# Gate and up products of two feed-forward blocks by Strassen's algorithm, with the gated features passed through DRAM

## The chip, the core and the metric

The kernel runs on one core of a Trainium2 chip. The core has a matrix engine (PE, whose weight loads have a row of their own, PEld), three engines for elementwise work (DVE, ACT and POOL) and a queue for transfers (SP); ACT and POOL issue transfers too. PE writes only to PSUM, and DVE or ACT bring its results to SBUF. The metric is the device time of one run in microseconds (us), the median of several runs.

## What is computed

One layer over 1056 tokens (1024 of a new stream and 32 of a running one), 1024 features wide. A feed-forward block (FFN) stands at either end of the layer and a token mixer between them.

```python
def rms_norm(x, w):
    xf = x.astype(jnp.float32)
    y = xf * lax.rsqrt(jnp.mean(xf * xf, axis=-1, keepdims=True) + RMS_EPS)
    return (y * w.astype(jnp.float32)).astype(x.dtype)
...
def swiglu(h, wg, wu, wd):
    return (jax.nn.silu(h @ wg) * (h @ wu)) @ wd
...
        x = x + 0.5 * swiglu(rms_norm(x, ffn1_norm[l]), ffn1_wg[l], ffn1_wu[l], ffn1_wd[l])
        ...
        x = x + mix.astype(x.dtype)
        x = x + 0.5 * swiglu(rms_norm(x, ffn2_norm[l]), ffn2_wg[l], ffn2_wu[l], ffn2_wd[l])
```

In each FFN, `wg` and `wu` are 1024 x 2816 and `wd` is 2816 x 1024, all in float32. The mixer (a delta rule, sliding-window attention and their projections) is not touched by the change, apart from the layout in which it gets and gives `x`.

## The kernel before

Features lie along the 128 partitions and tokens along the free dimension. The tokens are cut into three chunks of 352 (`CH`, `NC`), the 2816 hidden features into 22 tiles of 128. A float32 operand is written as the sum of two float32r parts (`split`, L158: ACT copies the high part, DVE subtracts it to get the low part), and a product takes three matmuls: high by high, high by low, low by high (L205, L206, L207 in `proj_g`). Weights come in units of 128 x 1024 (`unit_parts`, L147): a transfer on SP into one of two raw buffers `wr`, then the two parts `wh` and `wl`, three buffers each.

`ffn` (L320) goes over six blocks of four or three hidden tiles (`FF_BLOCKS`). In a block it makes, for each hidden tile and chunk, the gate product `pg` and the up product `pu` (8 x 3 matmuls of 352 columns each). A function `swiglu` then brings them to SBUF, gates them and splits the result into `gh` and `gl`. After that the block's down products are added to `x`: 8 output tiles by 3 chunks, each a group of w x 3 matmuls that ends in one DVE addition (L351). Gate, up and down products of a block thus follow each other, and the gated features never leave SBUF.

The norm costs PE no wait: `weigh` (L278) multiplies `x` by the norm's weight alone, and the tokens' factors 1/rms (`factors`, L288) are multiplied into the outputs of the products (`rb`, L334, L337). Before the first FFN the first chunk and the first weight unit are loaded in four pieces each, so that the products begin with the first piece.

PE's order is written by hand: what the code emits for PE runs in that order. The other engines' instructions are put in order by a scheduler, and each engine works off its own queue strictly in that order. `defer` and `tick` place the small matmuls of a norm so many product steps behind the place where they are asked for.

Of the kernel before, what the change touches and what calls it, by code (L numbers as in the profile page):

```python
# [14 lines left out]
P = 128  # L15
# [21 lines left out]
def unit_plan():  # L37
    """The order of the weight units in the packed weights, and the place of each."""
# [5 lines left out]
    def ffn(f):  # L44
        for (f0, w) in FF_BLOCKS:
            for m in range(f0, f0 + w):
                add((f, "g", m))
                add((f, "u", m))
            for u in range(w):
                add((f, "d", f0, u))  # L50
# [25 lines left out]
# columns of the tensors of small constants  # L76
# [27 lines left out]
def body(tc, wp, wba, xin, cst, mcst, bias, sconv, sdn, kcT, vc, y, dn_p, dn_s, convo, ko, vo, ko_s, vo_s):  # L104
# [4 lines left out]
    hp_ = ctx.enter_context(tc.tile_pool(name="hpool", bufs=1))  # L109
    pmm = ctx.enter_context(tc.tile_pool(name="pmm", bufs=3, space=PSUM))  # L110
    psm = ctx.enter_context(tc.tile_pool(name="psm", bufs=1, space=PSUM))
# [35 lines left out]
    def unit_parts(key, n):  # L147
        """The unit's parts of float32r, in n steps."""
# [20 lines left out]
    # work of the other engines behind a product, emitted a step at a time beside the next products  # L169
# [22 lines left out]
    first = []      # banks beside those of pmm, for the first products of all  # L192
    def proj_g(ws, hi, lo, c):
        """The product of the stationary tiles ws (unit, slot) with chunk c; yields between tiles."""
        if hi[0][c] is None:
            flush()
        bank = first.pop(0) if first else None
        if bank:
            ps = psm.tile([P, CH], F32, name=nm("pm"), tag=bank, bufs=1)
        else:  # L200
            ps = pmm.tile([P, CH], F32, name=nm("pm"), tag="pm")
# [28 lines left out]
    def squares(xc, tp, by):  # L230
        """The sum of the squares of the tiles xc, by the engines named: V with ACT, P alone, or both adding."""
# [17 lines left out]
    def rmsnorm(xc, wname, c, hi, lo, tp, n0, n1):  # L249
        """hi[k][c], lo[k][c] = the parts of RMSNorm of the chunk xc[k]."""  # L250
# [27 lines left out]
    def weigh(xc, wname, c, hi, lo, ks=range(KD)):  # L278
        """hi[k][c], lo[k][c] = the parts of x times the norm's weight."""
        wv = C(wname)  # L280
        for k in ks:
            hi[k][c], lo[k][c] = htile(F32R), htile(F32R)
            nc.scalar.activation(hi[k][c], xc[k], AF.Copy, scale=wv[:, k:k + 1])  # L283
            nc.vector.scalar_tensor_tensor(out=lo[k][c], in0=xc[k], scalar=wv[:, k:k + 1], in1=hi[k][c].bitcast(F32), op0=ALU.mult, op1=ALU.subtract)  # L284

    wait = {}       # by chunk, what follows its factors

    def factors(xc, c, tp, n0, n1, by):  # L288
        """The tile that gets the tokens' factors 1 / rms along the free dim, for the products' outputs."""
        rb = tp.tile([P, CH], F32, name=nm("rb"), tag="rb", bufs=NC)  # L290
        acc = squares(xc, tp, by)
        st = {}
        wait[c] = []

        def sums():
            ps = psm.tile([P, 4], F32, name=nm("pss"), tag="pc", bufs=2)
            for q in range(4):
                nc.tensor.matmul(out=ps[:QB, q:q + 1], lhsT=acc[:, q * QB:(q + 1) * QB], rhs=ones, start=True, stop=True)
            r = tp.tile([P, 4], F32, name=nm("r"), tag="r", bufs=2)
            nc.scalar.activation(r[:QB], ps[:QB], AF.Sqrt, scale=1.0 / (KD * P), bias=epst[:QB])  # L300
            nc.vector.reciprocal(r[:QB], r[:QB])
            st["r"] = r

        def spread():
            r = st["r"]
            pr = psm.tile([P, CH], F32, name=nm("pss"), tag="pd", bufs=1)
            for q in range(4):
                nc.tensor.matmul(out=pr[:, q * QB:(q + 1) * QB], lhsT=r[:QB, q:q + 1].to_broadcast([QB, P]), rhs=ident[:QB, :QB], start=True, stop=True)
            nc.scalar.activation(rb, pr, AF.Copy)
            for f in wait.pop(c):  # L310
                f()

        defer(n0, sums)
        defer(n1, spread)
        return rb

# [3 lines left out]
    def ffn(f, x, hi, lo, tp, gp, done, rb=None):  # L320
        """x += 0.5 SwiGLU(h); done(c) follows a chunk's last addition."""
        for bi, (f0, w) in enumerate(FF_BLOCKS):
# [29 lines left out]
            if not last:  # L352
                wds = []
                for d in range(KD):
                    while len(wds) * 8 < (d + 1) * w:
                        wds.append(load_unit((f, "d", f0, len(wds))))
# [899 lines left out]
```

## Time and profile before

| | |
|---|---|
| median of 3 runs | 2479.81 us (2479.49 to 2480.68) |
| span of the profiled execution | 2480.8 us |
| PE busy | 2459.2 us, 99% of the span, 15803 matmuls |
| PEld busy | 2401.1 us, 97% |
| DVE, ACT, POOL busy | 1094.3, 778.8, 284.5 us |
| float32r matmuls of 352 columns, gate and up of both FFNs | 6336 |
| the same, down products of both FFNs | 3168 |

Matmuls are pipelined, and their rows overlap in time: a row of 0.32 us does not mean that PE does one in 0.32 us. The pace is read from the distance of the starts. A span on POOL is rough.

### The profile page before, as it was taken

How to read it: one execution, taken by the hardware profiler on the slowest of the kernel's cores; microseconds unless marked ns; L12 is line 12 of the kernel's file. 1: busy time of each engine (PE TensorE's matmuls, PEld its weight loads, DVE VectorE, ACT ScalarE, POOL GpSimd, SP SyncE). 2: the span in 40 equal slices, each digit the busy share in tenths (PEclk: the TensorE clock that was granted, in tenths of full speed). 3: DMA queues.
4: the chain of work that ended last, by engine and by line, in shares of the span. 5: the costliest groups of instructions: out<-in, count | busy, mean ns of one | idle time of the engine just before them, and what ended most of it. 6: DMA issues, size and time to landing. Idle time of an engine off the chain costs nothing.

```text
span 2480.8 us, 37935 instructions
## 1 busy us (share of the span) xinstructions
PE 2459.2 (99%) x15803; PEld 2401.1 (97%) x15803; DVE 1094.3 (44%) x2471; ACT 778.8 (31%) x1483; POOL 284.5 (11%) x425
## 2 busy tenths in 40 slices
PE   8999999999999999999999999999999999999999
PEld 8999999999999989999888899999999999999999
DVE  5333333333437678765566632435233333333333
ACT  7212121111124655543586731315112111121111
POOL 0101010100014224222000000001101010010000
PEclk9999999999999999999999999999999999999999
DMA  3111111111113100010000021121111111111112
GB/s 133 52 52 36 51 52 43 43 52 43 52 35 118 54 26 20 21 32 20 20 27 27 27 74 52 35 100 41 43 52 43 52 43 44 42 52 43 52 36 86
DMA packets 34123, 119.24 MB, mean 48 GB/s; under 512 B 3792, under 2 KB 7200, under 8 KB 33568
## 3 DMA queue, kind: packets, MB, share of 16 engines
q1 hardware_dynamic: 31392, 104.97, 12.7%
q0 software_dynamic: 1696, 9.69, 1.0%
q8 instruction: 124, 2.03, 0.3%
q10 hardware_dynamic: 864, 2.16, 0.2%
q14 instruction: 47, 0.39, 0.0%
HBM read 107.43 MB, written 9.38 MB: 47 GB/s over the span
## 4 chain that ended last, share of the span: by engine, by line
PE 95%; DVE 2%; ACT 2%; issue 1%; DMA 0%; POOL 0%; POOLq 0%; ACTq 0%; SPq 0%; DVEq 0%
PE pm L205 29%; PE pm L207 28%; PE pm L206 28%; PE pss L682 1%; PE pss L690 1%; PE pss L1004 1%; PE pss L993 1%; PE pss L968 1%; PE pss L501 1%; PE pss L1044 1%; DVE tc L651 0%; ACT h L283 0%; ACT sq L241 0%; PE pss L736 0%; PE pss L724 0%
## 5 line engine op out<-in xcount | busy, mean ns | idle before, releaser
L205 PE MATMUL pm<-h,wh 128*128 128x352 f32 x3216 | 1061.6, 330 | 8.0 <-ACT wh L160 7.4
L207 PE MATMUL pm<-h,wl 128*128 128x352 f32 x3216 | 1039.7, 323 | 0.0
L206 PE MATMUL pm<-h,wh 128*128 128x352 f32 x3216 | 1037.7, 323 | 0.9 <-DVE h L284 0.9
L205 PEld LDWEIGHTS pm<-h,wh 128*128 128x128 f32 x3216 | 607.0, 189 | 14.7 <-ACT wh L160 7.4
L206 PEld LDWEIGHTS pm<-h,wh 128*128 128x128 f32 x3216 | 608.3, 189 | 3.2 <-DVE h L284 2.6
L207 PEld LDWEIGHTS pm<-h,wl 128*128 128x128 f32 x3216 | 605.0, 188 | 0.0
L160 ACT ACTIVATE wh<-wr 128x1024 fp32r<-128x1024 f32 (+1 forms) x190 | 197.6, 1042 | 662.2 <-PE pm L206 547.4
L205 PE MATMUL pm<-gh,wh 128*128 128x352 f32 x1056 | 341.9, 324 | 0.0
L207 PE MATMUL pm<-gh,wl 128*128 128x352 f32 x1056 | 340.2, 322 | 0.0
L206 PE MATMUL pm<-gl,wh 128*128 128x352 f32 x1056 | 340.0, 322 | 0.0
L161 DVE TENSOR_TENSOR wl<-wr,wh 128x1024 fp32r<-128x1024 f32 (+1 forms) x190 | 251.2, 1324 | 102.6 <-ACT wh L160 100.7
L338 POOL TENSOR_TENSOR s<-s,u 128x352 f32<-128x352 f32 x132 | 125.8, 953 | 1352.2 <-DVE u L337 1296.8
L351 DVE SCALAR_TENSOR_TENSOR x<-pm,x 128x352 f32<-128x352 f32 x288 | 149.9, 523 | 271.0 <-PE pm L207 271.0
L337 DVE TENSOR_TENSOR u<-pm,rb 128x352 f32<-128x352 f32 x132 | 69.2, 524 | 355.8 <-PE pm L207 355.8
L206 PEld LDWEIGHTS pm<-gl,wh 128*128 128x128 f32 x1056 | 199.0, 188 | 0.0
L207 PEld LDWEIGHTS pm<-gh,wl 128*128 128x128 f32 x1056 | 198.3, 188 | 0.0
L205 PEld LDWEIGHTS pm<-gh,wh 128*128 128x128 f32 x1056 | 198.2, 188 | 0.0
L160 ACT ACTIVATE gh<-s 128x352 fp32r<-128x352 f32 x132 | 65.8, 498 | 408.3 <-POOL s L338 408.3
L161 DVE TENSOR_TENSOR gl<-s,gh 128x352 fp32r<-128x352 f32 x132 | 68.8, 521 | 151.4 <-ACT gh L160 151.4
L334 DVE TENSOR_TENSOR s<-pm,rb 128x352 f32<-128x352 f32 x132 | 69.2, 524 | 139.2 <-PE pm L207 137.0
L335 ACT ACTIVATE s<-s 128x352 f32<-128x352 f32 x132 | 64.8, 492 | 200.8 <-DVE s L334 200.8
L546 DVE SCALAR_TENSOR_TENSOR row<-z,cs,row 128x352 f32<-128x352 f32 (+2 forms) x144 | 74.3, 540 | 12.3 <-ACT row L544 11.3
(259 smaller groups left out, 2068.6 us busy)
## 6 DMA issues: line engine op xcount, KB each, us to landing
wr<-wp SPq DMA_DIRECT2D x184, 512.0 KB, 3.4
xs<-x POOLq DMA_DIRECT2D x3, 1408.0 KB, 5.1
x<-xs POOLq DMA_DIRECT2D x6, 704.0 KB, 7.7
x<-xin SPq DMA_DIRECT2D x4, 704.0 KB, 7.7
x<-xin SPq DMA_DIRECT2D x4, 352.0 KB, 5.4
y<-x ACTq DMA_DIRECT2D x2, 704.0 KB, 3.1
y<-x SPq DMA_DIRECT2D x2, 704.0 KB, 3.1
y<-x ACTq DMA_DIRECT2D x4, 176.0 KB, 1.8
```

What stands on the lines that cost most here:

```text
L160: nc.scalar.activation(h, src, AF.Copy)
L161: (eng or nc.vector).tensor_tensor(out=l, in0=src, in1=h.bitcast(F32), op=ALU.subtract)
L205: nc.tensor.matmul(out=ps, lhsT=a, rhs=hi[k][c], start=k == 0, stop=False)
L206: nc.tensor.matmul(out=ps, lhsT=a, rhs=lo[k][c], start=False, stop=False)
L207: nc.tensor.matmul(out=ps, lhsT=b, rhs=hi[k][c], start=False, stop=k == n - 1)
L334: nc.vector.tensor_tensor(out=s, in0=pg, in1=rb[c], op=ALU.mult)
L335: nc.scalar.activation(s, s, AF.Silu)
L337: nc.vector.tensor_tensor(out=u, in0=pu, in1=rb[c], op=ALU.mult)
L338: nc.gpsimd.tensor_tensor(out=s, in0=s, in1=u, op=ALU.mult)
L351: nc.vector.scalar_tensor_tensor(out=x[d][c], in0=ps, scalar=0.5, in1=x[d][c], op0=ALU.mult, op1=ALU.add)
L501: nc.tensor.matmul(out=p1[p0:p0 + m, i, :], lhsT=src[:, o:o + m], rhs=w, start=True, stop=True)
L546: nc.vector.scalar_tensor_tensor(out=o, in0=z[:, z0 + i:z0 + i + m], scalar=cw[:, i:i + 1], in1=o, op0=ALU.mult, op1=ALU.add)
```

## The change

The 22 hidden tiles are taken in 11 pairs, the 1056 tokens in four quarters of 264 (`QT`), the 1024 input features in two halves. For a pair of tiles and a pair of quarters, the gate product is a product of 2 x 2 blocks (two hidden tiles by two halves; two halves by two quarters). For the pairs 1 to 10 it is made with 7 block products in place of 8, by Strassen's algorithm in Winograd's form; the up product likewise. The first pair is multiplied in the ordinary way while the quarters are still being normed.

Each FFN is now two phases. Phase one (`first_quarters`, `ffn_a`) makes all the gated features and stores them to DRAM (`gds`), from POOL's queue. Phase two (`ffn_b`) loads them again on SP, splits them and makes the down products as before, over seven blocks of 4, 3, 3, 3, 3, 3, 3 tiles. Differences of the weights' blocks (`pair_weights`) and of the tokens' quarters (`differences`) are made on DVE and POOL before the split; the additions behind the block products (`products`) are seven DVE instructions over 528 elements. The norm is applied to the quarters themselves before the products (`norm_quarter`); the factors on the outputs are gone. SBUF and PSUM pools are closed and opened anew between the phases, the second phase of the first FFN loads `x` again from the input, and the residual goes through a second DRAM copy (`xs2`) around phase one of the second FFN.

```diff
-FF_BLOCKS = [(0, 4), (4, 4), (8, 4), (12, 4), (16, 3), (19, 3)]
+FF_BLOCKS = [(0, 4)] + [(4 + 3 * i, 3) for i in range(6)]
+NJ = NF // 2
+QT = NT // 4
...
+    def pair_weights(f, j, s):
+        raw = pair_raw(f, j, s)
+        def tt(eng, out, a, b, op):
+            eng.tensor_tensor(out=raw[:, out], in0=raw[:, a], in1=raw[:, b], op=op)
+        a11, a12 = pair_parts(raw, (A11, A12))
+        tt(nc.vector, A11, A11, A21, ALU.subtract)
+        tt(nc.vector, S2, A22, A11, ALU.subtract)
+        tt(nc.gpsimd, A21, A21, A22, ALU.add)
+        s2, s1 = pair_parts(raw, (S2, A21))
+        tt(nc.gpsimd, A12, A12, S2, ALU.subtract)
+        s3, s4 = pair_parts(raw, (A11, A12))
+        a22, = pair_parts(raw, (A22,))
+        return dict(P1=a11, P2=a12, P6=s2, P5=s1, P7=s3, P3=s4, P4=a22)
...
+    def slot(w, hb, key):
+        wh, wl, o = w[key]
+        bank = pf.tile([P, 2, 512], F32, name=nm("pf"), tag="f")
+        for p in range(2):
+            for k in range(4):
+                a, b = wh[:, o + k * P:o + (k + 1) * P], wl[:, o + k * P:o + (k + 1) * P]
+                xh, xl = (t[:, k % 2, p, :] for t in hb[BLK[key]][k // 2])
+                out = bank[:, p, :QT]
+                nc.tensor.matmul(out=out, lhsT=a, rhs=xh, start=k == 0, stop=False)
+                nc.tensor.matmul(out=out, lhsT=a, rhs=xl, start=False, stop=False)
+                nc.tensor.matmul(out=out, lhsT=b, rhs=xh, start=False, stop=k == 3)
+                tick()
+        return bank[:, :, :QT]
...
+        t = slot(w, hb, "P1")
+        nc.scalar.activation(o[0][0], t, AF.Copy)
+        nc.scalar.activation(o[1][0], t, AF.Copy)
+        add(o[0][0], o[0][0], slot(w, hb, "P2"))
...
+        add(o[1][0], o[1][0], slot(w, hb, "P6"))
+        add(o[1][1], o[1][0], slot(w, hb, "P5"))
+        add(o[0][1], o[1][1], slot(w, hb, "P3"))
...
+        t = slot(w, hb, "P7")
+        add(o[1][0], o[1][0], t)
+        add(o[1][1], o[1][1], t)
...
+        add(o[1][0], o[1][0], slot(w, hb, "P4"))
...
+        for j in range(1, NJ):
+            g, u = outs(tp), outs(tp)
...
+            def up(m, h):
+                (nc.gpsimd if m == 0 else nc.vector).tensor_tensor(out=g[m][h], in0=g[m][h], in1=u[m][h], op=ALU.mult)
+                nc.gpsimd.dma_start(out=gd[2 * j + m, h], in_=g[m][h])
+            products(pair_weights(f, j, 0), hb, g, gate_)
+            products(pair_weights(f, j, 1), hb, u, up)
...
+                raw = gp.tile([P, NT], F32, name=nm("gr"), tag="gr", bufs=3)
+                for h in range(2):
+                    nc.sync.dma_start(out=raw.rearrange("p (a h t) -> p a h t", a=2, h=2)[:, :, h, :], in_=gd[f0 + m, h])
+                h, l = (gp.tile([P, NT], F32R, name=nm("gs"), tag="gs", bufs=11) for _ in range(2))
+                split(h, l, raw)
```

PE's queue inside the first FFN, before: gate and up products of 352 columns, high and low parts of `x` as `h`, of the weights as `wh` and `wl`.

```order
L205 MATMUL pm_245<-h_99,wh_94 128x352
L206 MATMUL pm_245<-h_100,wh_94 128x352
L207 MATMUL pm_245<-h_99,wl_95 128x352
L205 MATMUL pm_245<-h_103,wh_94 128x352
L206 MATMUL pm_245<-h_104,wh_94 128x352
L207 MATMUL pm_245<-h_103,wl_95 128x352
```

The same engine now, at the passage from block product P5 to P3 of the second pair (`hb` are the quarters' blocks and their differences, `pf` the PSUM tile of a block product).

```order
L421 MATMUL pf_930<-hb_122,wh_833 128x264
L422 MATMUL pf_930<-hb_123,wh_833 128x264
L423 MATMUL pf_930<-hb_122,wl_834 128x264
L421 MATMUL pf_956<-hb_128,wh_840 128x264
L422 MATMUL pf_956<-hb_129,wh_840 128x264
L423 MATMUL pf_956<-hb_128,wl_841 128x264
```

A matmul has three quarters of the columns, still with a weight load of its own; a pair's gate or up product is 168 of them (7 block products x 2 x 4 x 3), where it was 144 of 352 columns.

ACT's queue at the start of the program, before: the split of the first chunk (L283), squares for the norm (L241) and the split of the first unit (L160), mixed.

```order
L283 ACTIVATE h_99<-x_89,cs 128x352
L241 ACTIVATE sq_222<-x_89 128x352
L160 ACTIVATE wh_94<-wr_93 128x256
L283 ACTIVATE h_103<-x_89,cs 128x352
L241 ACTIVATE sq_224<-x_89 128x352
L283 ACTIVATE h_111<-x_89,cs 128x352
```

ACT's queue at the start now (`raw` are weight pieces as loaded, `t` the quarters of `x`, `hb` the normed and split quarter).

```order
L158 ACTIVATE wh_162<-raw_140 128x512 x2
L158 ACTIVATE wh_168<-raw_145 128x512 x2
L158 ACTIVATE wh_156<-raw_145 128x512
L550 DMA t_96<-xin 128x2x264
...
L550 DMA t_107<-xin 128x2x264
L346 ACTIVATE sq_186<-t_92 128x528
L346 ACTIVATE sq_188<-t_93 128x528
```

The split of eight weight pieces and the issue of twelve transfers of later quarters now stand ahead of the first square, and the first product needs the whole norm of the first quarter.

DVE's queue where the first FFN goes over from products to down products, before: `swiglu`'s L334 and L337, the last split of `gl`, then the additions of the down products.

```order
L334 TENSOR_TENSOR s_1083<-pm_1033,rb_438 128x352
L161 TENSOR_TENSOR wl_1185<-wr_1183,wh_1184 128x1024
L337 TENSOR_TENSOR u_1086<-pm_1058,rb_438 128x352
L161 TENSOR_TENSOR wl_1275<-wr_1273,wh_1274 128x1024
L161 TENSOR_TENSOR gl_1090<-s_1083,gh_1089 128x352
L351 SCALAR_TENSOR_TENSOR x_89<-pm_1099,x_89 128x352
```

DVE's queue now, at the joint of the two phases (`gr` are the gated features as loaded, `gs` their parts, `pf_5226` the last block product of phase one).

```order
L430 TENSOR_TENSOR t_4816<-t_4816,pf_5197 128x528
L430 TENSOR_TENSOR t_4817<-t_4817,pf_5197 128x528
L159 TENSOR_TENSOR wl_5406<-wr_5404,wh_5405 128x1024
L485 TENSOR_TENSOR t_4813<-t_4813,t_4817 128x528
L430 TENSOR_TENSOR t_4816<-t_4816,pf_5226 128x528
L159 TENSOR_TENSOR gs_5311<-gr_5307,gs_5310 128x1056
L485 TENSOR_TENSOR t_4812<-t_4812,t_4816 128x528
L159 TENSOR_TENSOR wl_5496<-wr_5494,wh_5495 128x1024
L505 SCALAR_TENSOR_TENSOR x_5274<-pm_5320,x_5274 128x352
```

The split of the fourth hidden tile of the first block (`gs_5311`) stands behind the addition of the last block product, so a part of the first down product's input comes after the end of phase one.

## Rows read from the trace of the kernel before

**Rows 1.** The page: busy time and share of the span, the chain of work that ended last by engine, and its first lines.

```profile
PE 2459.2 (99%) x15803; PEld 2401.1 (97%) x15803; DVE 1094.3 (44%) x2471; ACT 778.8 (31%) x1483; POOL 284.5 (11%) x425
...
PE 95%; DVE 2%; ACT 2%; issue 1%; DMA 0%; POOL 0%; POOLq 0%; ACTq 0%; SPq 0%; DVEq 0%
```

**Rows 2.** Groups of PE's matmuls by line and shape: busy time, mean ns of one, idle time before them and its releaser. `h` are gate, up and the mixer's products, `gh` and `gl` the down products.

```profile
L205 PE MATMUL pm<-h,wh 128*128 128x352 f32 x3216 | 1061.6, 330 | 8.0 <-ACT wh L160 7.4 <-DVE s L334 0.6
L207 PE MATMUL pm<-h,wl 128*128 128x352 f32 x3216 | 1039.7, 323 | 0.0
L206 PE MATMUL pm<-h,wh 128*128 128x352 f32 x3216 | 1037.7, 323 | 0.9 <-DVE h L284 0.9
L205 PE MATMUL pm<-gh,wh 128*128 128x352 f32 x1056 | 341.9, 324 | 0.0
```

**Rows 3.** Stretches of the span: start and end, length, busy time of PE, PEld, DVE, ACT and POOL with their instructions, granted clock, share of the transfer engines, GB/s.

```profile
0.00:100.00 100.00, 91.10 (x561) 88.67 (x562) 50.18 (x94) 52.00 (x97) 10.86 (x16) 1.00 0.30 104
200.00:400.00 200.00, 200.00 (x1248) 200.00 (x1247) 69.32 (x105) 36.85 (x55) 17.91 (x19) 1.00 0.14 48
```

**Rows 4.** Timeline of PE from 299.71 us on: start, length, line and shape; the first rows and the last row of one line.

```profile
299.87 0.33 PE L205 MATMUL pm<-h,wh 128*128 128x352 f32 x1
300.03 0.32 PE L206 MATMUL pm<-h,wh 128*128 128x352 f32 x1
300.19 0.32 PE L207 MATMUL pm<-h,wl 128*128 128x352 f32 x1
...
302.75 0.33 PE L205 MATMUL pm<-h,wh 128*128 128x352 f32 x1
```

**Rows 5.** Timeline of the weight loads at the same place.

```profile
299.87 0.19 PEld L206 LDWEIGHTS pm<-h,wh 128*128 128x128 f32 x1
300.04 0.19 PEld L207 LDWEIGHTS pm<-h,wl 128*128 128x128 f32 x1
300.19 0.19 PEld L205 LDWEIGHTS pm<-h,wh 128*128 128x128 f32 x1
```

**Rows 6.** Timeline of PE in the mixer: matmuls of 352 columns whose weights are 16 columns wide (128*16), the first and the last of a run of 15.

```profile
804.08 0.32 PE L450 MATMUL pss<-h,wb 128*16 128x352 f32 x1
...
806.33 0.32 PE L450 MATMUL pss<-h,wb 128*16 128x352 f32 x1
```

**Rows 7.** Timeline of PE around the small matmuls of one chunk's norm: eight with one moving column (weights 88 wide), later eight with 88 moving columns (weights 128 wide), each with the product that follows.

```profile
25.89 0.71 PE L298 MATMUL pss<-cs,acc 128*88 128x1 f32 x8
26.47 0.41 PE L205 MATMUL pm<-h,wh 128*128 128x352 f32 x1
...
31.81 1.02 PE L308 MATMUL pss<-cs,r 88*128 88x88 f32 x8
32.62 0.41 PE L205 MATMUL pm<-h,wh 128*128 128x352 f32 x1
```

**Rows 8.** Timeline of the first 14 us: SP's issues, ACT's and DVE's work on 512 columns, and PE's first product.

```profile
0.75 0.39 SPq L373 DMA_DIRECT2D x<-xin  x1
1.19 0.42 SPq L154 DMA_DIRECT2D wr<-wp  x1
...
7.40 0.66 PE L205 MATMUL pm<-h,wh 128*128 128x352 f32 x1 [7.40 <-ACT wh L160]
...
13.16 0.69 DVE L161 TENSOR_TENSOR wl<-wr,wh 128x512 fp32r<-128x512 f32 x1
13.22 0.62 ACT L160 ACTIVATE wh<-wr 128x512 fp32r<-128x512 f32 x1
```

**Rows 9.** Two of the same stretches as in Rows 3, shorter.

```profile
5.00:10.00 5.00, 2.60 (x9) 2.47 (x10) 3.14 (x7) 3.93 (x10) 0.00 (x0) 1.00 1.03 359
10.00:15.00 5.00, 4.65 (x19) 3.66 (x19) 5.00 (x12) 5.00 (x13) 0.00 (x0) 1.00 1.03 420
```

**Rows 10.** Groups of DVE, ACT and POOL by line and shape: busy time, mean ns of one, idle time before them and what ended it.

```profile
L351 DVE SCALAR_TENSOR_TENSOR x<-pm,x 128x352 f32<-128x352 f32 x288 | 149.9, 523 | 271.0 <-PE pm L207 271.0
L694 DVE TENSOR_TENSOR TT<-TT,pss 128x512 f32<-128x512 f32 x16 | 10.9, 684 | 8.9 <-PE pss L692 8.7
...
L160 ACT ACTIVATE gh<-s 128x352 fp32r<-128x352 f32 x132 | 65.8, 498 | 408.3 <-POOL s L338 408.3
L551 ACT ACT_TABLE_LOAD x11 | 14.1, 1283 | 0.2
...
L338 POOL TENSOR_TENSOR s<-s,u 128x352 f32<-128x352 f32 x132 | 125.8, 953 | 1352.2 <-DVE u L337 1296.8 <-ACT s L335 44.9 <-ACT wh L160 7.1
```

**Rows 11.** Timeline of DVE near the end of the second FFN: two splits of the same shape, the second of them beside a POOL instruction.

```profile
2439.72 1.23 DVE L161 TENSOR_TENSOR wl<-wr,wh 128x1024 fp32r<-128x1024 f32 x1 [0.41 <-ACT wh L160]
...
2443.66 1.74 DVE L161 TENSOR_TENSOR wl<-wr,wh 128x1024 fp32r<-128x1024 f32 x1 [0.46 <-ACT wh L160]
```

**Rows 12.** Transfers by line: queue, count, KB each, median us from issue to landing.

```profile
wr<-wp SPq DMA_DIRECT2D x184, 512.0 KB, 3.4
...
x<-xs POOLq DMA_DIRECT2D x6, 704.0 KB, 7.7
...
x<-xin SPq DMA_DIRECT2D x4, 352.0 KB, 5.4
```

**Rows 13.** Stretches as in Rows 3, at the end of the first FFN and at the beginning of the second one's products.

```profile
780.00:800.00 20.00, 18.86 (x117) 18.57 (x116) 17.90 (x36) 9.63 (x22) 14.35 (x23) 0.95 0.49 166
...
1680.00:1700.00 20.00, 20.00 (x134) 20.00 (x132) 13.83 (x28) 15.38 (x31) 3.96 (x4) 1.00 0.00 0
```

More of the change, by code (lines that the diff above doesn't have):

```diff
@@ L196, in proj_g @@
             flush()
[L197 to L201, printed above, removed]
+        ps = pmm.tile([P, CH], F32, name=nm("pm"), tag="pm")
         n = len(ws)
@@ L276, in rmsnorm @@
         defer(n1, scale)
[L278 to L315, printed above, removed]
@@ new lines, in qdiff, with differences @@
+    def qdiff(xq, out, a, b):
+        for i in range(2):
+            eng = nc.gpsimd if i else nc.vector
+            eng.tensor_tensor(out=xq[out[0]][out[1] + i], in0=xq[a[0]][a[1] + i], in1=xq[b[0]][b[1] + i], op=ALU.subtract)
+    def differences(hb, xq, p):
+        q, r = 2 * p, 2 * p + 1
+        qdiff(xq, (q, 0), (r, 0), (q, 0))
+        qdiff(xq, (r, 0), (r, 2), (r, 0))
+        qdiff(xq, (r, 2), (r, 2), (q, 0))
+        qdiff(xq, (q, 2), (q, 2), (r, 2))
+        qparts(hb, xq, "T1", q, 0, "VP")
+        qparts(hb, xq, "T4", q, 2, "VP")
+        qparts(hb, xq, "T3", r, 0, "VP")
@@ new lines, in starter, with start, then, rest @@
+    def starter(hb, xq, wname, tp):
+        def start(q, n0, n1, late=None):
+            def then():
+                qparts(hb, xq, "T2" if q % 2 else "B11", q, 0)
+                if late is not None:
+                    late.append(rest)
+                else:
+                    rest()
+            def rest():
+                qparts(hb, xq, "B22" if q % 2 else "B21", q, 2)
+                if q % 2:
+                    differences(hb, xq, q // 2)
+            norm_quarter(xq[q], wname, tp, n0, n1, then)
+        return start
@@ L359, in ffn @@
             else:
[L360 removed]
+                wds = [load_unit((f + 1, "d", f0, u)) for u in range(w)]
                 for c in range(NC):
@@ new lines, in body, with fetch_q @@
+    st_w, wqp = pool("wqa1")
+    st_v, wqb = pool("wqb1")
+    st_t, tp = pool("t1", "right")
+    st_p, pf = pool("pf1", space=PSUM, bufs=3)
+    st_n, psn = pool("pn1", space=PSUM)
+    psn_tags, psn_bufs = ("na", "nb"), (1, 1)
+    xq = quarters(tp)
+    hb = {}
+    new_blocks(hb, wqp, ("B11", "B21", "T2"))
+    new_blocks(hb, wqb, ("T1", "T3", "B22", "T4"))
+    def fetch_q(q):
+        for a in range(4):
+            nc.scalar.dma_start(out=xq[q][a], in_=xin[a][:, :, q * QT:(q + 1) * QT])
@@ new lines, in body @@
+    fetch_q(0)
+    fw = first_weights(0)
+    for q in range(1, 4):
+        fetch_q(q)
+    start = starter(hb, xq, "n1", tp)
+    start(0, 0, 0)
+    flush()
+    first_quarters(fw, hb, xq, tp, gds[0], lambda q: start(q + 1, 4, 11) if q < 3 else None)
+    ffn_a(0, hb, tp, gds[0])
+    st_n.close()
+    st_p.close()
+    st_t.close()
+    st_v.close()
+    st_w.close()
+    st_h, hp_ = pool("hpool", "right")
+    st_p, pmm = pool("pmm1", space=PSUM, bufs=3)
+    st_n, psm = pool("psm1", space=PSUM)
@@ L1121, in body @@
     ws = [load_unit(("out", d)) for d in (5, 6, 7)]
-    rb = []
+    psn, psn_tags, psn_bufs = psm, ("pc", "pd"), (2, 1)
+    late = []
+    begin = starter(hb, xq, "n3", tp)
     for c in range(NC):
```

275 lines of the change are left out of this document (186 added, 89 removed).

## The prediction

> **What bounds the kernel now.** I read the page's totals first: PE is busy 99% of the span and makes up 95% of the chain that ended last [rows 1]. Then the groups of PE by shape: in the feed-forward blocks the idle time before matmuls is a few microseconds in all [rows 2], and a stretch of 200 us holds 1248 matmuls with PE and its weight loads busy throughout, while DVE is at 35% and ACT at 18% [rows 3]. So the time is the number of matmuls times their pace. The pace is not the 323 ns of a row but the distance of the starts: from 299.87 to 302.75 us there are 18 matmuls of 352 columns, 160.0 ns each [rows 4], at a granted clock of 1.00, which is the level of 2.4 GHz [rows 3]. The last question is what the 160.0 ns consist of, since the change alters the width. A matmul whose weights are only 16 columns wide keeps the same pace (14 steps in 2.25 us, 161 ns) [rows 6]: the weight load does not set it. One column per cycle at 2.4 GHz would be 352 / 2.4 = 146.7 ns, so 13.3 ns are left over, either a fixed sum per matmul or something that grows with the columns. The trace of before can't tell which, as all its float32r matmuls have 352 columns.
>
> **The products.** Removed: gate and up of both FFNs, 2 x 44 x 8 x 3 x 3 = 6336 matmuls x 160.0 ns = 1013.8 us. Added: a pair's gate or up product takes 7 block products x 2 x 4 x 3 = 168 matmuls, ten pairs x 2 x 168 = 3360 in an FFN, and the first pair in the ordinary way 4 quarters x 96 = 384; for two FFNs 7488 matmuls of 264 columns. Their pace is the largest unknown. If the left-over 13.3 ns are fixed, it is 264 / 2.4 + 13.3 = 123.3 ns and the sum 923.3 us; if all of it goes with the columns, 264 / 352 x 160.0 = 120.0 ns and 898.6 us. The nearest rows with short matmuls give a floor: eight with 88 moving columns and 128 weight columns take 0.81 us, some 101 to 108 ns each [rows 7], below both. I take the middle, 121.7 ns and 911.3 us, since nothing decides: **-102.5 us** (-115.2 to -90.5).
>
> The Trainium skill speaks against this change: its page Perfetto Trace Analysis, section Identifying the Most-Contended Engine, judges PE's headroom by the busy share of the weight loads. Here that is 97%, and the change raises the loads from 6336 to 7488; what that would give is the second rival below. The page TensorE: Matmul & The Clock Gate, section Back-to-back issue gap, gives the width over 2.4 GHz plus 2.5 ns; by it the 264-column sum would be 842 us, but it also gives 149.2 ns for 352 columns, where the rows have 160.0, so I don't use it.
>
> **What runs beside phase one.** For each gate or up product of a pair (168 x 121.7 = 20.4 us of PE), DVE does 7 splits and 2 differences of 512 elements at 0.69 us [rows 8], and 7 additions from PSUM of 528, a little over the 0.684 us of a 512-element one [rows 10], say 0.70: 6.2 + 4.9 = 11.1 us, and 0.7 us of gating on average. ACT does 7 copies at 0.62 us and 4 more of 528: 7 us. POOL makes 2 block sums, about 1.4 us each by 953 ns for 352 elements [rows 10], and on average one gating product. All are under PE's 20.4 us, and weights of the next product can be split while this one runs, since there are three buffers. A DVE split beside POOL took 1.74 us instead of 1.23 [rows 11]; were everything on DVE slower by that ratio, it would have 16.7 us of work, still covered. The stores to DRAM (1.1 MB a pair) and loads of weights (2.1 MB a pair, in 41 us) are small against 359 GB/s [rows 9]. I count nothing; if the cover is gone, it is the third rival.
>
> **The start.** Before, the first product begins at 7.40 us [rows 8]. By 100 us 513 products and 48 small matmuls have run [rows 3]; at 160.0 ns, and 0.58 and 0.81 us for eight small ones [rows 7], that is 86.3 us of work, so 13.7 us are lost. Now the first product needs the complete norm of a quarter, and ACT's queue puts other things first. Eight weight pieces and the quarter, 3.2 MB, come at the 359 to 420 GB/s of this stretch [rows 9] by about 12 us; the last of the eight splits ends near 13. Twelve issues at 0.44 us [rows 8] make 5 us, and since later ones wait for the landing of earlier ones (5.4 us for a similar piece [rows 12]), the squares begin at 18 to 21 us. Then in sequence: four squares with their additions 5 us, a table load of 1.28 us [rows 10], root, reciprocal and small matmuls 2.5 us, eight scalings on DVE at 0.43 us (by 523 ns for 352 columns [rows 10]) 3.4 us, the first split 1.3 us: the first products run at 31 to 34 us, and the first quarter's go at DVE's pace of splits for some 4 us more. In all about 35 us are lost against 13.7: **+21 us**. Bounds: 27 lost if the transfers don't delay ACT, 45 if DVE and ACT, which have to norm, split and subtract each later quarter in the 11.7 us of PE's work on the one before, keep PE waiting as well: +13 to +31.
>
> **The norms' small matmuls.** Per quarter 12 with one column and 6 that spread, 1.5 us by [rows 7], eight quarters 12.4 us; before six chunks at 1.4 us, 8.4 us: **+4 us**.
>
> **The joints of the phases.** The first down product needs a PSUM bank that the last addition of phase one empties, and the fourth tile's split stands behind that addition on DVE: 0.7 + 1.4 us, and the queue ahead of it. I take 2 us for each FFN, **+4 us** (0 to 12; the upper end is one load of `x` at 7.7 us [rows 12] that comes late because POOL issues it behind the last stores, less the first products' 1.9 us each).
>
> **The second FFN's start.** Before, PE does not idle there [rows 13]. Now the quarters' norms run beside the output projection; at its end DVE still has eight scalings and two splits ahead of the additions that empty the banks, about 2.5 us, and the gating of the first quarter's products waits for the differences, since both use the same tiles: **+5 us** (0 to 12).
>
> **The rest.** Down products are the same 3168 matmuls; at a block's end the split of the next tile's low part has 1.1 to 1.6 us before it is needed and takes 1.3, about even. The mixer's start, where PE already loses about 1 us and the clock is at 0.95 [rows 13], gets four stores on POOL for each chunk instead of one: **+2 us** (0 to 5).
>
> **The sum.** 2480.8 - 102.5 + 21 + 4 + 4 + 5 + 2 = 2414.3 us of span; the median is 1.0 us under the profiled span, so **2413 us**. With all the low ends 2382, with all the high ends 2453.
>
> **Rivals.**
> First, *the pace is right but the edges cost more*: the norms at the starts and the joints lose PE more than the high ends say. DVE's work for two quarters (16 scalings, 8 to 16 splits, additions, differences) comes near the 24 us that PE takes for them. If it takes half as much again at both starts, 12 us each, the sum is about 2437, and with the high ends of the rest 2465. Chance 0.10 above my range.
>
> Second, *the weight load sets the pace*, and fewer columns don't help. For it speaks that PEld is busy 97% [rows 1] and a load's row is 0.19 us long, more than the pace [rows 5]. Against it speak the loads 16 columns wide at the same pace [rows 6] and the small matmuls at some 105 ns with full loads [rows 7]; a load also begins before the one ahead has ended [rows 5]. If a load and its matmul took 160 ns whatever the width, phase one would be 7488 x 160.0 = 1198.1 us, and the time 2480.8 + 184.3 + 36 - 1 = 2700. The change loses from a pace of (1013.8 - 36) / 7488 = 130.6 ns on. Chance 0.06. The skill's rule on load busy time is this case, and the trace of before bears it out little.
>
> Third, *DVE is late inside phase one*: a block product's bank must be emptied within two products, 5.9 us, but DVE's queue also holds splits that wait for weight buffers. A wait of 1 us in each of 2 x 20 products costs 40 us (2453), 2.5 us costs 100 us and takes the gain away (2513). Against it stand the 11.8 us of work in 20.4. Chance 0.05, half of it at or above the time before.
>
> Fourth, *everything costs less*: the proportional pace and a start at its low end, under 2382. Chance 0.02.
>
> **How the numbers follow.** My forecast, 2413 us, has 0.77 within 2382 to 2453; above it lie the first rival (0.10), the second (0.06) and the third (0.05), below it the fourth (0.02). The range is 2382 to 2453. A measurement of this kernel tells 0.2%, about 5 us, from no change. Faster by more than that holds for the forecast, the first and fourth rivals and half of the third: 0.91; within 0.2%: 0.02; slower: 0.07.
>
> **What would show it.** In the profile of the changed kernel, the starts of 264-column matmuls should be 120 to 123 ns apart in the middle of phase one, with PE busy throughout; a pace of 131 or more would make the prediction wrong in sign. The first product should begin at 31 to 34 us. At the two joints PE should idle about 2 us each with DVE's split or addition as the releaser, and in the first 50 us of both phases one the waits should name DVE and ACT. DVE should be busy some 60% of phase one. Waits on DVE spread evenly through phase one would be the third rival.

## The result, and the profile after

| | us | ratio to before, 95% interval |
|---|---|---|
| before, measured beside it | 2480.17 (median of 4) | 1 |
| after | 2448.57 (2446.24 to 2450.5, 4 runs) | 0.9873 [0.9859, 0.9887] |
| the profiled execution of after | span 2446.0 | |
| forecast | 2413 (2382 to 2453) | |

The change gains 31.6 us where 67 were forecast; the time lies in the range, 36 us above its likeliest value. The page of after, totals, two lines of slices and the chain, answers to [rows 1]:

```profile
span 2446.0 us, 41679 instructions
...
PE 2373.2 (97%) x17003; PEld 2314.3 (95%) x17003; DVE 1348.5 (55%) x2888; ACT 886.7 (36%) x1639; POOL 466.9 (19%) x571
...
PE   4899999999999999999999999999999999999999
...
PEclk9899999999999999999999999999999999999999
...
PE 91%; DVE 4%; ACT 1%; DMA 1%; issue 1%; POOL 1%; SPq 0%; ACTq 0%; DVEq 0%; POOLq 0%
```

DVE has 4% of the chain that ended last instead of 2%, and PE's first two slices (61 us each) are not full. Stretches of after (start and end, length, busy time of PE, PEld, DVE, ACT, POOL with their instructions, granted clock, transfers' share, GB/s) answer to [rows 3]:

```profile
0.00:140.00 140.00, 96.17 (x716) 94.92 (x717) 76.34 (x127) 58.45 (x99) 36.19 (x30) 0.95 0.27 92
60.00:80.00 20.00, 11.85 (x81) 11.66 (x81) 12.22 (x24) 12.45 (x21) 4.12 (x4) 0.81 0.00 1
80.00:100.00 20.00, 19.82 (x144) 19.86 (x145) 12.87 (x19) 6.59 (x11) 9.30 (x6) 0.84 0.05 18
300.00:400.00 100.00, 100.00 (x820) 100.00 (x819) 53.93 (x85) 30.36 (x52) 30.88 (x28) 1.00 0.24 86
520.00:540.00 20.00, 18.16 (x103) 18.19 (x104) 11.11 (x16) 3.31 (x4) 4.78 (x9) 0.91 1.01 375
1700.00:1720.00 20.00, 13.18 (x75) 12.71 (x75) 15.03 (x29) 8.22 (x16) 8.77 (x6) 0.77 0.36 134
1720.00:1740.00 20.00, 20.00 (x154) 20.00 (x153) 14.82 (x24) 10.03 (x17) 5.74 (x4) 0.88 0.00 1
```

The same first 140 us of the kernel before:

```profile
0.00:140.00 140.00, 131.10 (x811) 128.67 (x812) 65.72 (x118) 57.62 (x104) 12.76 (x18) 1.00 0.26 89
```

TensorE idles 43.8 us there instead of 8.9, and what it does it does at a mean clock of 0.95. In the middle of phase one nothing is lost. PE's timeline of after, two of its early products first, then what answers to [rows 4]:

```profile
38.56 0.42 PE L396 MATMUL pf<-hb,wr 128*128 128x264 f32 x1
38.78 0.42 PE L397 MATMUL pf<-hb,wr 128*128 128x264 f32 x1
...
299.68 0.28 PE L421 MATMUL pf<-hb,wh 128*128 128x264 f32 x1
299.80 0.29 PE L422 MATMUL pf<-hb,wh 128*128 128x264 f32 x1
299.92 0.28 PE L423 MATMUL pf<-hb,wl 128*128 128x264 f32 x1
...
302.97 0.29 PE L421 MATMUL pf<-hb,wh 128*128 128x264 f32 x1
...
518.82 0.29 PE L423 MATMUL pf<-hb,wl 128*128 128x264 f32 x1
521.84 0.40 PE L198 MATMUL pm<-gs,wh 128*128 128x352 f32 x1 [2.73 <-DVE t L430]
```

From 299.68 to 302.97 there are 27 steps, 121.9 ns each (forecast 121.7); by the 820 matmuls of 100 us it is 122.0. The early two are 220 ns apart. The last two rows are the first joint: phase one ends at 519.1, and the first down product waits 2.73 us for an addition on DVE. PE's waits of after in the first 130 us, by what it waited for (us in all, times, the longest):

```profile
PE pss L357 <- DVE sq L350: 33.0, 2, 29.9
PE pss L366 <- DVE r L360: 6.1, 2, 5.5
PE pf L397 <- DVE hb L159: 1.8, 1, 1.8
PE pf L396 <- ACT hb L158: 1.7, 1, 1.7
```

And ACT's timeline there (an ACTq row is the issue of transfers):

```profile
10.83 2.71 ACT L158 ACTIVATE wh<-raw 128x512 fp32r<-128x512 f32 x5 [0.48 <-DMA raw<-wq]
13.45 0.55 ACTq L550 DMA_DIRECT2D t<-xin  x1
...
14.04 11.01 ACTq L550 DMA_DIRECT2D t<-xin  x11
25.09 1.18 ACT L346 ACTIVATE sq<-t 128x528 f32<-128x528 f32 x2 [11.02 <-issue]
...
55.37 1.28 ACT L472 ACT_TABLE_LOAD   x1
61.55 0.39 ACT L472 ACTIVATE t<-pf 128x264 f32<-128x264 f32 x1 [4.89 <-POOL hb L159]
...
64.59 0.26 ACT L359 ACTIVATE r<-pss,epst 88x3 f32<-88x3 f32 x1
```

Two places are to be seen. Eleven issues hold ACT for 11.01 us ahead of the first square, so that the first sum reaches TensorE at 29.90. And the first Silu (L472), whose output takes the buffer of a quarter still being subtracted, waits until 61.55 for POOL; the root of the third quarter (L359) is queued behind it, and TensorE waits 5.5 us for its reciprocal.

### The profile page after: what moved, and what is told of

The parts are those of the page before. It is cut to its first block, busy times and chain, and to the rows that moved or that the text cites. A ratio compares the mean times of both kernels' runs of the same rounds, so it can differ in the third digit from the quotient of the medians.

```text
span 2446.0 us, 41679 instructions
## 1 busy us (share of the span) xinstructions
PE 2373.2 (97%) x17003; PEld 2314.3 (95%) x17003; DVE 1348.5 (55%) x2888; ACT 886.7 (36%) x1639; POOL 466.9 (19%) x571
## 4 chain that ended last, share of the span: by engine, by line
PE 91%; DVE 4%; ACT 1%; DMA 1%; issue 1%; POOL 1%; SPq 0%; ACTq 0%; DVEq 0%; POOLq 0%
PE pm L198 15%; PE pm L199 15%; PE pm L200 15%; PE pf L423 11%; PE pf L421 11%; PE pf L422 11%; PE pf L396 1%; PE pf L397 1%; PE pss L852 1%; PE pf L398 1%; PE pss L860 1%; PE pss L1174 1%; PE pss L1163 1%; PE pss L1138 1%; PE pss L671 1%
## 5 line engine op out<-in xcount | busy, mean ns | idle before, releaser
L423 PE MATMUL pf<-hb,wl 128*128 128x264 f32 x2240 | 641.2, 286 | 0.0
L421 PE MATMUL pf<-hb,wh 128*128 128x264 f32 x2240 | 637.1, 284 | 1.3 <-DVE t L473 1.3
L422 PE MATMUL pf<-hb,wh 128*128 128x264 f32 x2240 | 637.8, 285 | 0.0
L421 PEld LDWEIGHTS pf<-hb,wh 128*128 128x128 f32 x2240 | 423.3, 189 | 1.6 <-DVE t L473 1.6
L422 PEld LDWEIGHTS pf<-hb,wh 128*128 128x128 f32 x2240 | 420.9, 188 | 0.0
L423 PEld LDWEIGHTS pf<-hb,wl 128*128 128x128 f32 x2240 | 420.8, 188 | 0.0
L198 PE MATMUL pm<-h,wh 128*128 128x352 f32 x1104 | 372.7, 338 | 1.9 <-DVE t L1293 1.9
L200 PE MATMUL pm<-h,wl 128*128 128x352 f32 x1104 | 357.2, 324 | 0.0
L199 PE MATMUL pm<-h,wh 128*128 128x352 f32 x1104 | 357.1, 323 | 0.0
L198 PE MATMUL pm<-gs,wh 128*128 128x352 f32 x1056 | 344.2, 326 | 7.4 <-DVE t L430 5.2
L199 PE MATMUL pm<-gs,wh 128*128 128x352 f32 x1056 | 342.5, 324 | 0.0
L198 PEld LDWEIGHTS pm<-h,wh 128*128 128x128 f32 x1104 | 208.6, 189 | 8.9 <-issue 6.5
L199 PEld LDWEIGHTS pm<-h,wh 128*128 128x128 f32 x1104 | 208.6, 189 | 0.2
L200 PEld LDWEIGHTS pm<-h,wl 128*128 128x128 f32 x1104 | 208.0, 188 | 0.0
L198 PEld LDWEIGHTS pm<-gs,wh 128*128 128x128 f32 x1056 | 199.9, 189 | 8.0 <-issue 5.5
L199 PEld LDWEIGHTS pm<-gs,wh 128*128 128x128 f32 x1056 | 200.4, 190 | 0.4 <-DVE gs L159 0.4
```

Of the source, the lines that this page charges most:

```text
L198: nc.tensor.matmul(out=ps, lhsT=a, rhs=hi[k][c], start=k == 0, stop=False)
L199: nc.tensor.matmul(out=ps, lhsT=a, rhs=lo[k][c], start=False, stop=False)
L200: nc.tensor.matmul(out=ps, lhsT=b, rhs=hi[k][c], start=False, stop=k == n - 1)
L421: nc.tensor.matmul(out=out, lhsT=a, rhs=xh, start=k == 0, stop=False)
L422: nc.tensor.matmul(out=out, lhsT=a, rhs=xl, start=False, stop=False)
L423: nc.tensor.matmul(out=out, lhsT=b, rhs=xh, start=False, stop=k == 3)
```

## Experiments

The theory (A in the texts below): the pace gives what was forecast, and the missing time lies at the edges, chiefly at the first FFN's start. The rivals: something inside phase one, or a start that is set by other work whatever is moved. Ratios are to the kernel before, run beside each, and differences between runs are taken from them; 0.001 is 2.5 us.

**q_on_sp.**

```diff
-            nc.scalar.dma_start(out=xq[q][a], in_=...)
+            (nc.sync if q else nc.scalar).dma_start(out=xq[q][a], in_=...)
```

> The twelve transfers of x's quarters 1 to 3 are issued by SP behind the first weights, instead of by ACT. Theory A (the 35 us that the forecast lacks lie at the edges, first of all where ACT issues these twelve from 14.04 to 25.05 us of the span ahead of its first square): the squares begin some 11 us earlier, the first product at about 25 us instead of 35.6, and the time falls by 8 to 11 us, to 2437 to 2441. Rival B (x's or the weights' arrival, or DVE's own work, sets the first product, and ACT only fills a wait): the time stays within 2 us of 2448.6. Rival C (the loss is in the pace inside phase one): no change either.

2437.6 us, ratio 0.9826 [0.9812, 0.9839]: 11.7 us less than after. ACT's timeline in it:

```profile
11.21 3.27 ACT L158 ACTIVATE wh<-raw 128x512 fp32r<-128x512 f32 x6 [0.33 <-DMA raw<-wq]
14.38 1.16 ACT L346 ACTIVATE sq<-t 128x528 f32<-128x528 f32 x2
```

The squares follow the splits at once, 10.7 us earlier; the first product stands at 24.89 instead of 35.61. So the issues stood on the path. Phase one ends 8.6 us earlier, at 510.5 instead of 519.1; some 1 us went into more products at the slow pace of 220 ns. On SP the same twelve issues take 8.74 us, from 9.51 on, behind the first weights.

**own_out**, the store of this piece being its own too:

```diff
-                o = g[m][q % 2][:, q // 2, :]
+                o = g[m][q % 2][:, q // 2, :] if q else spare.pop(0)
```

> The first quarter's gated outputs (two tiles of 128x264) go into an unused part of the two raw weight tiles, so that ACT's Silu waits no longer until the differences on POOL have read the quarter whose buffer it reuses. Theory A: ACT's idle 4.89 us before 61.55 us goes, the root behind it comes earlier, TensorE's gap of 5.50 us at 65.20 us and the clock of 0.81 in the stretch 60 to 80 go with it: 6 to 10 us less, 2439 to 2443; the second FFN's start, which has the same order, gives 0 to 3 more. Rival B (the wait is taken over by the next one on DVE, whose queue is full there): less than 3 us.

2443.52 us, ratio 0.9848 [0.9834, 0.9861], 6.2 us less than after, with intervals that just meet. That seems to confirm A, but the trace does not: PE's waits in the first 130 us read

```profile
PE pss L357 <- DVE sq L350: 35.1, 3, 26.5
PE pss L366 <- DVE r L360: 0.6, 1, 0.6
```

The 5.5 us wait for the reciprocal has gone, and the other waits for a sum of squares grew from 3.1 us (33.0 - 29.9) to 8.6 (35.1 - 26.5). The wait moved one step up DVE's queue, as rival B said. What was gained there, 3.4 us, is that the first sum came at 26.5 instead of 29.9, because the same eleven issues took 7.25 us in this execution and not 11.01.

**both.**

> Both edits together: the quarters 1 to 3 issued by SP, and buffers of their own for the first quarter's gated outputs. Theory A: the two add up, 14 to 21 us less than 2448.6, so 2428 to 2435. Rival B (one chain of DVE and POOL work runs from the first square to the last difference, so that an earlier beginning only makes a longer wait behind it): the sum is worth no more than the larger of the two alone, 2438 or above.

2435.25 us, ratio 0.9815 [0.9802, 0.9829]. Beside q_on_sp the difference is 2.7 us and the intervals overlap; PE is busy 106.85 us of the first 140 in this one and 106.84 in that. So the two don't add up, and the buffers are worth little: rival B.

**eight.**

```diff
-            products(pair_weights(f, j, 0), hb, g, gate_)
-            products(pair_weights(f, j, 1), hb, u, up)
+            for s, done in ((0, gated), (1, upped)):
+                raw = pair_raw(f, j, s)
+                w = [pair_parts(raw, bs) for bs in ((A11, A12), (A21, A22))]
+                for m in range(2):
+                    for h in range(2):
+                        done(m, h, slot8(w[m], hb, h))
```

> The pairs behind the first of each FFN get their four outputs by ordinary products, eight blocks instead of seven, with the same two phases, quarters, stores and starts (the block T2 keeps x12; the differences of x are still made, for nothing). 960 products of 264 columns more at 122.0 ns are 117.1 us. Theory A (Strassen's sums of outputs and weights on DVE cost TensorE nothing inside phase one; the loss is in the layout's edges): 2562 to 2568, that is 85 us above the kernel before. Rival C (the sums hold TensorE up inside phase one, in many small waits): the ordinary products gain some of that back, 2540 to 2555.

2591.39 us, ratio 1.0444 [1.0430, 1.0459]: 141.6 us more than after, 24.5 above the 117.1 of the products and above what either theory gave. Two stretches of it, in the middle of phase one and at its first joint, and two of its waits:

```profile
300.00:400.00 100.00, 100.00 (x821) 100.00 (x820) 17.38 (x26) 15.32 (x27) 4.32 (x8) 1.00 0.19 65
580.00:590.00 10.00, 1.62 (x3) 0.79 (x3) 1.26 (x1) 1.08 (x1) 0.00 (x0) 0.50 1.04 405
```

```profile
PE pm L198 <- ACT gs L158: 24.8, 5, 10.2
PE pm L199 <- DVE gs L159: 6.0, 8, 1.0
```

With DVE at 17% TensorE does 821 matmuls in 100 us; with Strassen's sums, DVE at 54% in the same stretch of after, it does 820. So the sums cost TensorE nothing there, and rival C falls. What is left over is mostly at the joints: 30.8 us of waits for the gated features read back from DRAM, where after's joints wait 5.2. The transfers run at 405 GB/s there, `x` among them. SP issues these loads late: from 564.65 us, 8 us before the end of phase one, where after issues them from 500.80, 18 us before it; in both, SP had waited for a block product. That the buffers come free later because the products end in another order is likely, but was not tried.

**no_norm.**

```diff
-            norm_quarter(xq[q], wname, tp, n0, n1, then)
+            if wname == "n1":
+                defer(n1, then)
+            else:
+                norm_quarter(xq[q], wname, tp, n0, n1, then)
```

> On top of both: the first FFN's normalisation is left out (its 12 small matmuls per quarter, squares, roots and scalings are not done; the quarters of x are split as they land; the second FFN keeps its own). It bounds from below what the first FFN's start can give. Theory A (the chain square, sum, root, spread, scale, split stands ahead of the first quarter and comes again ahead of each of the next three): the first product stands at 14 to 16 us of the span instead of 27.2, the gaps of 5.5 and 3.1 us and the lower clock after them go, and some 10 us of small matmuls: 27 to 38 us less than both, 2398 to 2408. Rival B (the differences and splits on DVE and POOL hold the start by themselves): 13 us or less, 2422 or above.

2411.76 us, ratio 0.9721 [0.9708, 0.9735]: 23.3 us less than both, a little short of A's 27 to 38 and far from B's 13. PE's first product and the first 140 us:

```profile
15.03 0.59 PE L399 MATMUL pf<-hb,wr 128*128 128x264 f32 x1 [15.03 <-ACT hb L158]
```

```profile
0.00:140.00 140.00, 119.91 (x933) 118.87 (x934) 78.28 (x110) 52.87 (x95) 46.91 (x40) 0.98 0.32 109
```

PE is busy 13.1 us more there than in both, at 0.98 instead of 0.95, and has no small matmuls to do. Phase one ends at 483.8 us instead of 510.4, so the 54 us that both needs beyond its products' 456.8 become 27. The norm ahead of the quarters is thus half of what the start costs; of the 20 us that stay idle 15 lie ahead of the first product, while weights and `x` arrive and are split.

**all3, best and mixed** move the differences: in all3 all to DVE, in best also the first splits between the scalings, in mixed to DVE in the first FFN alone.

```diff
-            eng = nc.gpsimd if i else nc.vector
+            eng = nc.vector                                  # all3, best
+            eng = nc.gpsimd if i and second else nc.vector   # mixed
```

> On top of both: the differences of the quarters run on DVE alone instead of half on POOL, where three in a row took 5.15 us from 42.74 us and DVE's own beside them 1.83 and 1.93 us instead of 0.69. Theory A (POOL's share holds DVE's queue and so the squares' sum that TensorE waits for 5.50 us at 52.03 us): the eight differences take 5.5 us on DVE, the gap falls by 2 to 4 us, the second pair's by 0 to 2, and the clock's fall behind it is shorter: 3 to 7 us less than both, 2428 to 2432. Rival B (DVE's queue is as long either way): within 2 us of both.

> On top of all3: the splits of a quarter's first half come after four of its eight scalings instead of after all eight. Theory A: the first product waits no longer for the last four scalings on DVE (its second matmul stood at 27.23 us, the first at 24.89): 1 to 2 us less at the first FFN's start and as much at the second's, so 2 to 4 us below all3, 2425 to 2429. Rival B (the wait passes to the second half's splits): 0 to 1 us.

> On top of both: the differences run on DVE alone in the first FFN, and half on POOL in the second as they were. In all3 the waits for the squares' sum in the first FFN's start fell (PE busy 110.05 us of the first 140 instead of 106.85), but the second FFN's grew from 5.5 to 8.0 us. Theory A (the two cancelled): the first FFN's gain is kept, 3 to 7 us less than both, 2428 to 2432. Rival B (the edges' time is not additive, or all3's gain in the first 140 us was lost elsewhere in the first FFN): within 2 us of both, 2433 to 2437.

all3 2434.04 us, 0.9811 [0.9798, 0.9824]; best 2434.9, 0.9815 [0.9801, 0.9828]; mixed 2432.14, 0.9802 [0.9789, 0.9815]. None can be told from both. In all3 the eight differences did take 5.03 us on DVE and PE was busy 110.05 us of the first 140, but the second FFN's longest wait for squares grew from 5.5 to 8.0 us: each start has DVE's queue full in its own way. In best the second FFN's stayed 8.0; the second product came at 25.79 us instead of 27.25, but the waits for squares behind the first grew from 6.8 to 9.0 us and took it back. Mixed keeps the first FFN's side (110.22 us) and lies between A and B.

**later.**

```diff
-    ... start(q + 1, 4, 11) ...   begin(q + 2, 4, 11) ...
+    ... start(q + 1, 12, 20) ...  begin(q + 2, 12, 20) ...
```

> On top of mixed: inside the first quarters' products TensorE meets the next quarter's small matmuls after 12 and 20 steps of three products instead of after 4 and 11, in both FFNs. Theory A (TensorE stands waiting for a squares' sum with products of the quarter before still to do, and its clock falls for it): the waits on the squares' sum behind the first (6.8 us in the first FFN's start, 5.5 and more in the second's) shrink by most of the 8 steps, 2.9 us, each: 4 to 10 us less than mixed, 2420 to 2426. Rival B (the scalings and splits behind the small matmuls then come as much later, and the next quarter's first product waits instead): 0, or a few us more.

2432.62 us, 0.9807 [0.9794, 0.9821]: no change from mixed. The second FFN's waits for squares fell from 7.0 us in two to 4.5 in three; in the first FFN 9.6 us of such waits (28.9 - 19.3) stood behind the first, where mixed has 6.8 (25.8 - 19.0). What one start gained the other lost.

**warm_gap and warm.**

```diff
+            nc.tensor.matmul(out=pr[:, :DW], lhsT=dum[0][:, :P], rhs=dum[0], start=True, stop=True)
+    fill = {("n1", 2): 50, ("n3", 2): 50}                      # warm_gap
+    fill = {("n1", 2): 50, ("n3", 2): 50, ("n1", 0): 95}       # warm
```

> On top of mixed: 50 idle products of 160 columns (their result is not used) stand on TensorE ahead of the two sums of squares that it waited for: in mixed 6.52 us at 52.92 us of the span, with a granted clock of 0.52 in the ten microseconds behind, and 5.52 us at 1700.24, with 0.71 behind. At some 111 ns they take 5.5 us, about what the waits take. Theory A (a wait costs itself and then as much again, because the clock falls behind it): the granted clock stays at 1.00 there, 10 x 0.48 + 10 x 0.29 = 7.7 us at the most are saved, 4 to 8 us less than mixed: 2424 to 2428. Rival B (the clock behind such a wait hides under the later waits for DVE's scalings and splits): within 2 us of mixed. Rival C (the idle products come in the way): slower.

> On top of warm_gap: 95 such products also run before the first sum of squares, from about 4 us of the span on, while the weights and x arrive. In mixed the first 40 products of 264 columns were 220 ns apart instead of 122, until about 36 us. Theory A (they are slow because TensorE did nothing before): 40 x 0.098 = 3.9 us less than warm_gap. Rival B (the next quarter's norm on DVE sets that stretch, or the idle 8 us of small matmuls and waits between undo the warming): 0 to 1 us.

warm_gap 2430.67 us, 0.9795 [0.9781, 0.9808]; the interval overlaps mixed's. The place itself went as A says. The same ten microseconds in mixed, then in warm_gap:

```profile
50.00:60.00 10.00, 7.08 (x36) 7.12 (x37) 4.98 (x6) 4.54 (x7) 3.48 (x4) 0.52 0.62 238
```

```profile
50.00:60.00 10.00, 9.07 (x81) 8.91 (x80) 7.01 (x13) 5.90 (x9) 3.30 (x4) 1.00 0.63 239
```

In mixed TensorE had waited 6.52 us until 52.92; then the granted clock was 0.52, nearly all of it the level of 1.2 GHz, and it did 36 matmuls, 21 of them products. With the wait filled it stayed at 1.00 and did 81, of which 16 were idle ones and 53 products. The low level itself cost mixed some 3.5 us, an estimate from the starts: 21 products 220 ns apart instead of 122, and two groups of small matmuls 0.8 and 0.5 us longer. That is half of the wait, not as much again. In the second FFN the filling only moved the wait (3.0 us for a reciprocal, clock 0.66 from 1700 to 1710), and the sum of both can't be told from mixed. warm is slower, 2438.52, 0.9832 [0.9818, 0.9845]: its 95 products took 216 ns each, ran until 28.08 us and so delayed the first sum. A's 3.9 us did not come: the first products were 220 ns apart all the same, until 43.0 us. (There are some 30 of them, 32 in both, and not 40.)

The idle products in warm_gap, then those at the start of warm:

```profile
45.97 5.71 PE L348 MATMUL pss<-dum 128*128 128x160 f32 x50
```

```profile
7.53 20.55 PE L348 MATMUL pss<-dum 128*128 128x160 f32 x95 [7.53 <-ACT dum L565]
```

**half.**

```diff
+                e = QT if k in (0, 3) else QT // 2
```

> Of the 24 matmuls of a Strassen product 12 take 132 columns instead of 264 (the right half of their contribution is left out), 3360 of the 6720 in all; weights and everything else stay. The two kinds of pace are told apart by this: with a fixed sum of 12 ns beside the columns a narrow one takes 67 ns and the time falls by 3360 x 55 = 185 us, to about 2264, as far as DVE keeps up; if the pace grows in proportion, 61 ns and 2244; if a weight load needs the 105 ns of the small matmuls with full loads, a narrow one takes 105 ns and the time falls by only 57 us, to about 2392.

2417.89 us (one execution): 31 us less than after, where a fixed sum would have given 185 and a load of 105 ns 57. A stretch of it, and PE's timeline with wide and narrow products:

```profile
300.00:400.00 100.00, 100.00 (x860) 100.00 (x859) 56.77 (x90) 31.60 (x54) 29.27 (x27) 1.00 0.23 83
```

```profile
300.12 0.28 PE L424 MATMUL pf<-hb,wl 128*128 128x264 f32 x1
300.24 0.23 PE L422 MATMUL pf<-hb,wh 128*128 128x132 f32 x1
300.31 0.27 PE L423 MATMUL pf<-hb,wh 128*128 128x132 f32 x1
300.42 0.28 PE L424 MATMUL pf<-hb,wl 128*128 128x132 f32 x1
300.53 0.28 PE L422 MATMUL pf<-hb,wh 128*128 128x132 f32 x1
300.64 0.28 PE L423 MATMUL pf<-hb,wh 128*128 128x132 f32 x1
300.75 0.27 PE L424 MATMUL pf<-hb,wl 128*128 128x132 f32 x1
```

Narrow products stand 110 ns apart once the run of them has begun, with half the columns, PE and PEld full and no wait. Over the stretch a product takes 116.3 ns on average, wide and narrow, instead of 122.0: 38 us over the 6720, of which the joints take 6 back (11.6 us of waits instead of 5.2). The idle products of 160 columns in warm_gap took 114 ns at the most (5.71 / 50), so between 132 and 160 columns the pace hardly moves. A product with its own weight load thus has a floor near 110 ns, and 264 columns at 122.0 are only 12 ns above it. That the load sets this floor is argued and not tested: small matmuls take 73 ns with weights 88 wide and 101 with weights 128 wide [rows 7], but no run changed the width of the weights alone. The Trainium skill, TensorE: Matmul & The Clock Gate, section Back-to-back issue gap, says that in a stream of loads and products both set the spacing, about 81 ns at 128 columns; the formula that the prediction takes from there is the page's for an isolated product. This run fits the first and has 110 ns at 132 columns of float32r.

## Why the prediction was right and wrong

**Products: right.** Forecast -102.5 us at 121.7 ns; 7488 x 122.0 = 913.5 instead of 1013.8, -100.3. Between a leftover in proportion (120.0) and a fixed one (123.3) the 122.0 do not decide. The second rival was right that there is a floor, at another height: not 160 ns, but by half near 110, 12 ns below 264 columns' pace. The Trainium skill, Perfetto Trace Analysis, section Identifying the Most-Contended Engine, judges headroom by the loads' busy share; after's 95% and these 12 ns agree, while at 352 columns, with 97%, narrower products still gained 38 ns each.

**DVE beside phase one: right.** DVE is busy 54% of the stretch above (forecast some 60), PE is busy all of it, and eight shows the same pace without the sums. The third rival is out.

**The start: the step that failed**, a term that was mis-sized. The first FFN's phase one ends at 519.1; its 3744 products at 122.0 ns are 456.8, so 62 us went to waits, lower clock and the norm's small matmuls. The prediction had 35 lost and half of 12.4 for the small ones, 41: **21 us too little**. By the starts of PE's rows the 62 are 43.8 us of idle time and some 7 us of products at 220 ns instead of 122 (together 51, where 35 were counted), and some 10 us of small matmuls, which run slow as well (where 6.2 were counted). Three of its numbers were off. Twelve issues were to take 5 us and the squares to begin at 18 to 21; they took 11.6 and the squares began at 25.09 (q_on_sp shows that this was on the path: the first product came 10.7 us earlier without them, the end of phase one 8.6). The first products were to run at 31 to 34 us; they ran at 35.61 and 37.95. And behind them 4 us were counted; the waits there are 5.5, 3.1 and 1.3 us, and the pace behind a wait was carried by no term: the clock was 0.81 and 0.84 between 60 and 100 us, and the first products ran 220 ns apart until 45.1 us. The bounds, 27 to 45 lost, were too low as well: their upper end allowed for DVE being late, not for slow products behind it.

**The second FFN's start: mis-sized too.** Forecast +5. From the first product at 1710.29 to the wait of 2.44 us ahead of 2185.99 it takes 473.3 us, 16.5 over 456.8, of which two quarters' small matmuls were to be 3; with the two waits of 1.32 and 1.43 us before it, some 16. **11 us too little**, with 5.50 us of one wait and clocks of 0.77 and 0.88 in the rows above.

**The joints: right in place and releaser.** 2.73 and 2.44 us with DVE's addition as releaser, forecast 2 each. Behind each, nine to eleven products ran 290 ns apart instead of 160 (the clock of 0.91 above), which is some 1.4 us more and was in no term.

**The sum.** 21 + 11 + 1 + 2 = 35 us above the forecast span of 2414.3, 38 with the slow products at the joints, where 31.7 were measured; the other 3 to 6 are not resolved, in the rest or in the estimate of what before loses. So the mechanism of the first rival, *edges cost more* (2437, up to 2465), is what happened. Its 0.10 stood for a time above the range, which did not come. That the range held is luck in part: both starts lay beyond their bounds (56 us lost against 45, 16 against 12), and the products, the joints and the rest stayed below their high ends. The direction did not hang on it.

What stays open: why eleven issues on ACT took 11.01 us in one execution and 7.25 in another, why the first products ran at half pace, what sets the floor of 110 ns, and what the second FFN's start could give.

## What to carry to other kernels

Price an edge by its chain, not by its busy times: every norm, split and subtraction that must be done before the first product is a serial chain over three engines, and it came back for each quarter. A wait of several microseconds on TensorE costs more than itself, by the lower clock behind it: some 3.5 us for 6.5 of wait in mixed. And look for a floor before a matmul is made narrower: from 352 to 264 columns 38 ns were gained, but a second level of Strassen that halves the columns again would, by these rows, put 49 products of 132 columns in the place of 28 of 264, an estimate of 49 x 110 = 5.4 us against 28 x 122.0 = 3.4. A second level need not do so: a block here is two matmuls of 264 columns side by side, and one that takes a single quarter and hidden tiles in fours keeps the 264. That was not tried.

Of the kernels that compute all, mixed (2432.14) and warm_gap (2430.67) are the fastest, 0.980 of before; the two can't be told apart. About two thirds of what they have over after (17.6 and 19.3 us) is q_on_sp's one line (11.7). no_norm's 23 us bound what the first FFN's norm could still give; whether its factors can come behind the first products was not tried.

## What the runs showed of the hardware

- In a run of float32r products, each with a weight load of its own, the starts are 110 ns apart at 132 columns (half), 122.0 at 264 (after) and 160.0 at 352 (before); idle products of 160 columns took at most 114 (warm_gap).
- The first some 30 products of 264 columns of a run stood 220 ns apart (27.62 to 36.3 us in both), though the granted clock of that stretch is given as 1.00; in warm, after 20 us of products on constants, it was so until 43.0 us.
- Three subtractions of 528 elements on POOL took 7.89 us beside DVE in after, and 5.15 in both, where a single one takes 1.33.
- Twelve transfers of 264 KB hold the queue that issues them for 11.6 us on ACT (after) and 8.74 on SP (q_on_sp); the first of them alone took 0.55.
